# First pass of a decoder trunk on one core: scale's dot product ahead of shift's, weight low parts in two pieces, squares summed by TensorE

## The chip, the cores and the metric

One core of a Trainium2 chip runs the whole program in one launch. The metric is the device time in microseconds (us). Engines are named as the profile names them: PE is TensorE's matmul, PEld its weight load, DVE is VectorE, ACT is ScalarE, POOL is GpSimd, SP is SyncE, which here issues nearly all transfers.

## The reference

Two decoder layers over 256 tokens of width 1024, each a token mixer and a gated ConvFFN. Every sub-layer takes a normed and modulated input `h`, and the change concerns the first of them:

```
mod = silu(c) @ w_ada[i] + b_ada[i]
sh1, sc1, g1, sh2, sc2, g2 = split(mod, 6)
h = rmsnorm(x, norm_mix[i]) * (1.0 + sc1) + sh1
y = dilated_mixture(h, w_in_a, w_out_a, rel_bias)      # starts with h @ w_in_a
```

So before the first projection can start, the kernel needs the root mean square of x, and, for each of eight slices of 128 channels, a shift and a scale, which are dot products of `silu(c)` with 128 columns of `w_ada` each.

## The kernel before

Channels lie on partitions. `x`, `h` and all activations are kept as eight tiles (kt = 0 to 7) of 128 channels by 256 tokens. For accuracy every float32 product of the projections is made as three: operand a is split into a high part (ScalarE's copy into the type fp32r) and a low part (VectorE's subtraction a - high), and `mm3` issues high*high, high*low and low*high into the same accumulator.

The first pass is the projection that makes q, k and v of the first two head pairs. For it, each tile kt brings two transfers, both into the pool `wraw` (four buffers shared by all kinds of weights, so a load waits until the load four places earlier has been used up):

- `ada_chunk(0, kt)` (L130 to L151): 1 MB of `w_ada`, which holds the shift weights of tile kt in its first half and the scale weights in its second (`ADA_ORDER`, L51). Two VectorE dot products (L138), each followed by a small ScalarE activation that makes the column `mod` (shift at L148, scale at L146).
- `split(I["w0"][kt])` (L156 to L170): 0.96 MB of projection weights, 1920 columns. ScalarE copies two halves of 960 columns into `whi` (L165), then VectorE subtracts twice into `wlo` (L169). `wspl` has three buffers of each.

`normed` (L250 to L263) makes h for a tile: VectorE multiplies x by scale and the reciprocal root `rstd` (`xr`, L257), ScalarE adds the shift (`hhi`, L259), VectorE makes `hlo` (L260). TensorE then does for that tile 42 matmuls: 18 of 256 columns for the first head pair (`pqk`, weight columns 0 to 767), 6 of 384 columns for v (columns 768 to 1151, which span both halves), and 18 for the second head pair (columns 1152 to 1919).

Ahead of that stand the squares of x: VectorE squares tiles 0 to 3 (L354), ScalarE tiles 4 to 7 (L357), VectorE adds each four to one by two additions (L360), and `rstd_of` (L183 to L192) sums the two over channels with two matmuls by a matrix of ones (`ms`, L187), then ln and exp on ScalarE (L189, L191). `keep_warm` (L266 to L270) issues matmuls whose result nobody reads.

Each engine runs its own queue strictly in the order in which the program was laid out. A scheduler lays it out from the order of the code and its own estimate of times; `with behind(i)` makes it place what follows after instruction i on its engine. For the tiles from 2 on VectorE's queue is: two dots of tile kt+1, `hlo` of tile kt, both low parts of tile kt+1, `xr` of tile kt+1.

After the pass come the second pair's v (`pv`, weights `in_wv`), the attention of pair 0, and so on.

Of the kernel before, what the change touches and what calls it, by code (L numbers as in the profile page):

```python
# [57 lines left out]
def trunk(ctx: ExitStack, tc: tile.TileContext, I, out):  # L58
# [40 lines left out]
    def col(at):  # L99
        return small[:, at : at + 1]  # L100
# [25 lines left out]

    mod = {}

    def ada_chunk(l, n, dmas=1):
        raw = wraw.tile([P, 2048], F32, tag="raw", name="ada_raw")  # L130
        for i in range(dmas):
            c = slice(2048 * i // dmas, 2048 * (i + 1) // dmas)
            nc.sync.dma_start(raw[:, c], I["w_ada"][l, n][:, c])
        for s in range(2):
            piece, kt = ADA_ORDER[2 * n + s]
            dot = tmp.tile([P, 1], F32, tag="dot", name="dot", bufs=4)
            w = raw[:, D * s : D * s + D]
            nc.vector.tensor_tensor_reduce(  # L138
                w, w, c_bc, op0=ALU.mult, op1=ALU.add, scale=1.0, scalar=0.0, accum_out=dot,
            )  # L140
            m = state.tile([P, 1], F32, tag=f"mod{l}{piece}{kt}", name="mod")
            b = col(C_BADA + 48 * l + 8 * piece + kt)
            if piece in (1, 4):
                g = col((C_NMIX if piece == 1 else C_NFFN) + 8 * l + kt)
                b1 = (16 if piece == 4 else 0) + 8 * l + kt
                last = nc.scalar.activation(m, dot, AF.Identity, scale=g, bias=one_b[:, b1 : b1 + 1])  # L146
            else:
                last = nc.scalar.activation(m, dot, AF.Identity, bias=b)  # L148
            mod[l, piece, kt] = m
        return last  # L150


    last_load, copied, last_lo = [None], [None], [None]

    def split(src, n, dmas=1, after=((), ()), late=(), low=()):
        raw = wraw.tile([P, 2048], F32, tag="raw", name="raw")  # L156
        for i in range(dmas):
            c = slice(n * i // dmas, n * (i + 1) // dmas)
            last_load[0] = nc.sync.dma_start(raw[:, c], src[:, c])
        hi = wspl.tile([P, 2048], F32R, tag="whi", name="whi")  # L160
        lo = wspl.tile([P, 2048], F32R, tag="wlo", name="wlo")
        for i in range(0, n, n // 2):
            c = slice(i, i + n // 2)
            with behind(*after[i > 0]):
                copied[0] = nc.scalar.copy(hi[:, c], raw[:, c])  # L165
        for i in range(0, n, n // 2):
            c = slice(i, i + n // 2)
            with behind(*(late if i else low)):
                last_lo[0] = nc.vector.tensor_tensor(lo[:, c], raw[:, c], hi[:, c].bitcast(F32), op=ALU.subtract)  # L169
        return hi, lo  # L170

    def mm3(ps, a, b, start, stop):

# [76 lines left out]
                st.enter_context(tc.issue_after(i.ins))  # L250
            yield

    def normed(l, sub, r, kt):

        xr = tmp.tile([P, T], F32, tag="xr", name="xr")
        a, sh = mod[l, 3 * sub + 1, kt], mod[l, 3 * sub, kt]
        nc.vector.scalar_tensor_tensor(xr, x[kt], a[:, 0:1], r, op0=ALU.mult, op1=ALU.mult)  # L257
        hi, lo = h_hi[kt][:, :], h_lo[kt][:, :]
        i = nc.scalar.activation(hi, xr, AF.Identity, bias=sh[:, 0:1])  # L259
        j = nc.vector.scalar_tensor_tensor(  # L260
            lo, xr, sh[:, 0:1], hi.bitcast(F32), op0=ALU.add, op1=ALU.subtract
        )
        chain[kt] = chain[7] = i, j  # L263
        return h_hi[kt], h_lo[kt]

# [60 lines left out]
    def parts(w, at, n=P):  # L326
        return w[0][:, at : at + n], w[1][:, at : at + n]
# [27 lines left out]
    with behind(silu):  # L355
        for i in (4, 6):
            last_sq = nc.scalar.activation(sq[:, i : i + 2, :], x_all[:, i : i + 2, :], AF.Square)  # L357
    for n in (0, 4):
        for m in (2, 1):
            last_add = nc.vector.tensor_tensor(sq[:, n : n + m, :], sq[:, n : n + m, :], sq[:, n + m : n + 2 * m, :], op=ALU.add)  # L360
        if n == 0:
            with behind(last_add):
                last_add = scale_terms(0)
    exp_ln_after(last_sq)
    r = rstd_of([sq[:, 0, :], sq[:, 4, :]])

    rows_ps, at = [], 0
    with behind(norm_ops[0]):
        keep_warm(3)
        for i, (g, n) in enumerate(ROWS):  # L370
            c = slice(at, at + n)
            ps = bank("rows", "t")[:16, 0:n]
            rows_ps.append((ps, c))
            mm(ps, tab[:, 16 * g : 16 * g + 16], oh[:33, c], start=True, stop=True)
            at += n
    first = norm_ops[1], last_add
    w0, h = [], []
    for kt in range(KT):
        with behind(*first):
            term = ada_chunk(0, kt, dmas=1 if kt else 2)  # L380
        h.append(normed(0, 0, r, kt))
        if kt:
            w0.append(split(I["w0"][kt], 15 * P))
        else:
            with behind(chain[0][1]):
                w0.append(split(I["w0"][kt], 15 * P, 2, after=((term,), (chain[0][0],))))
# [3 lines left out]
            first = (last_lo[0],)  # L390
        if kt == 1:
            scale_terms(1)
    with tc.issue_after(last_load[0].ins):
        nc.sync.dma_start(x_all, I["xT"])
        nc.sync.dma_start(rows_d, rows)
# [109 lines left out]
    for u in range(NPAIR):  # L505
        with tc.issue_after(last_load[0].ins):
            bias = load_bias(u)
        q = [q_pair[u % 2]]
        k = [[att.tile([P, T + 4], F32R, tag=f"k0{i}", name="k") for i in range(2)]]
        for z in k[0]:  # L510
            nc.gpsimd.memset(z[:, T:].bitcast(F32), 0.0)
        for g in (1, 2):
            q.append(att.tile([P, T], F32, tag=f"q{g}", name="q"))
            k.append(att.tile([P, T], F32, tag=f"k{g}", name="k"))
        v = [att.tile([P, NG * P], F32, tag=f"v{t}", name="v") for t in range(2)]
        if u == 0:
            b0 = [bank("pqk", tg) for tg in "ssspp"]
            pqk = [b[:, T * i : T * i + T] for b in b0[:3] for i in range(2)]
            pv = b0[3:]
            b1 = [bank("pqk", "t") for _ in range(3)]  # L520
            pqk1 = [b[:, T * i : T * i + T] for b in b1 for i in range(2)]
            for kt in range(KT):
                s, e = kt == 0, kt == KT - 1
                for i in range(2 * NG):
                    mm3(pqk[i][:, :T], parts(w0[kt], P * i), h[kt], s and i % 2 == 0, e and i % 2 == 1)
                wv = parts(w0[kt], 6 * P, NG * P)
                for t in range(2):
                    ht = [y[:, P * t : P * t + P] for y in h[kt]]
                    mm3(pv[t][:, : NG * P], ht, wv, s, e)
                for i in range(2 * NG):  # L530
                    mm3(pqk1[i], parts(w0[kt], 9 * P + P * i), h[kt], s and i % 2 == 0, e and i % 2 == 1)
        if u < 2:
            for g in range(NG):
                evacuate(q, k, g, (pqk, pqk1)[u][2 * g], (pqk, pqk1)[u][2 * g + 1])
        else:
            for g in range(NG):
                w = split(I["wqk"][u - 2, g], 2048)
                pqk = bank("pqk", "p")
                pq, pk = pqk[:, :T], pqk[:, T:]
                for kt in range(KT):  # L540
                    s, e = kt == 0, kt == KT - 1
                    mm3(pq[:, :T], parts(w, 2 * P * kt), h[kt], s, False)
                    mm3(pk[:, :T], parts(w, 2 * P * kt + P), h[kt], False, e)
                with behind(evacuate(q, k, g, pq, pk)):
                    next_ada()
        if u > 0:
            pv = [bank("pv", "p") for _ in range(2)]
            for half in range(2):
                with behind(*chain[7]):
                    w = split(I["wv"][u - 1, half], 1536)  # L550
                for k4 in range(4):
                    kt = 4 * half + k4
                    wv = parts(w, 384 * k4, 384)
                    for t in range(2):
                        ht = [y[:, P * t : P * t + P] for y in h[kt]]
                        mm3(pv[t][:, :384], ht, wv, kt == 0, kt == KT - 1)
        for n in range(2):
            by_group(v[n], pv[n], n)
        attend(u, q, k, v, bias)
        if u == 1:  # L560
            for n in range(2):
                next_ada()
# [506 lines left out]
```

## Time and profile before

| | |
|---|---|
| median of three runs | 788.61 us |
| the three runs | 788.61, 790.08, 784.72 us |
| the profiled execution: its time | 784.46 us |
| its span | 782.7 us |
| its mean granted TensorE clock | 0.997 |

| engine | busy us | share of the span |
|---|---|---|
| PEld | 741.9 | 95% |
| DVE | 643.2 | 82% |
| ACT | 480.2 | 61% |
| POOL | 14.4 | 2% |

A share is an average over the whole span; the stage that the change touches lies in its first 60 us and has to be read by itself. In the rows of a timeline the first number is the start, the second the duration, then engine, line, operation, output and input; what stands in brackets is the idle time of the engine before it and what ended it. Vector and scalar instructions overlap a little at their ends, so what one costs its queue is the distance between starts, not the duration.

### The profile page before, as it was taken

The numbers are of one execution on the slowest core, as the hardware profiler recorded it, in microseconds if no ns is written. First come the engines' busy times: TensorE is split into PE (matmuls) and PEld (weight loads), VectorE is DVE, ScalarE is ACT, GpSimd is POOL, SyncE is SP. The second block draws the span as 40 slices with busy tenths as digits, with TensorE's granted clock in tenths as the row PEclk, the third lists the DMA queues.
The fourth block names the chain that finished last, engine by engine and source line by source line (L and its number), as shares of the span: only waits on it lengthen the run. The fifth ranks groups of instructions, "written<-read, shape, count | busy, mean of one in ns | idle before, by whom it ended". The sixth has DMA issues, their size and how long they took to land.

```text
span 782.7 us, 15883 instructions
## 1 busy us (share of the span) xinstructions
PE 769.9 (98%) x6416; PEld 741.9 (95%) x6416; DVE 643.2 (82%) x1160; ACT 480.2 (61%) x936; POOL 14.4 (2%) x40
## 2 busy tenths in 40 slices
PE   8999999999999999999999999999999999999997
PEld 6899999999999999999999999898999999999997
DVE  6998978878779758999998976797568898899762
ACT  5566555545645557867666656664667866667552
POOL 1000000000000010000000100000010000000000
PEclk9999999999999999999999999999999999999999
DMA  9998577585785736777645994966445765556741
GB/s 349 417 325 350 191 287 272 195 323 193 264 299 194 266 103 250 247 268 265 227 144 206 322 341 152 340 241 229 144 144 185 252 211 173 207 182 208 262 158 54
DMA packets 32616, 184.72 MB, mean 236 GB/s; under 512 B 5852, under 2 KB 7388, under 8 KB 16286
## 3 DMA queue, kind: packets, MB, share of 16 engines
q1 hardware_dynamic: 32160, 183.26, 65.4%
q8 instruction: 50, 0.82, 0.4%
q10 hardware_dynamic: 382, 0.45, 0.2%
q14 instruction: 24, 0.20, 0.1%
HBM read 182.59 MB, written 1.10 MB: 235 GB/s over the span
## 4 chain that ended last, share of the span: by engine, by line
PE 74%; DVE 11%; DMA 8%; ACT 4%; issue 2%; ACTq 0%; DVEq 0%
PE pab L176 10%; PE pab L175 10%; PE pab L177 10%; PE pd L177 5%; PE pd L176 5%; PE pd L175 5%; DMA raw<-in_wqk 5%; DVE wlo L169 4%; PE pqk L177 3%; PE pqk L176 3%; PE pqk L175 3%; DMA raw<-in_wv 3%; DVE ada_raw L138 2%; PE py L175 2%; PE py L177 2%
## 5 line engine op out<-in xcount | busy, mean ns | idle before, releaser
L169 DVE TENSOR_TENSOR wlo<-raw,whi 128x1024 fp32r<-128x1024 f32 (+3 forms) x274 | 291.8, 1096 | 52.5 <-ACT whi L165 51.8
L165 ACT CAST whi<-raw 128x1024 fp32r<-128x1024 f32 (+3 forms) x274 | 245.5, 945 | 135.3 <-PE pab L176 40.4
L177 PE MATMUL pab<-hhi,wlo 128*128 128x256 f32 x672 | 184.7, 276 | 0.0
L176 PE MATMUL pab<-hlo,whi 128*128 128x256 f32 x672 | 184.6, 276 | 0.0
L175 PE MATMUL pab<-hhi,whi 128*128 128x256 f32 x672 | 183.2, 277 | 0.0
L176 PEld LDWEIGHTS pab<-hlo,whi 128*128 128x128 f32 x672 | 126.0, 188 | 0.2
L177 PEld LDWEIGHTS pab<-hhi,wlo 128*128 128x128 f32 x672 | 126.1, 188 | 0.0
L175 PEld LDWEIGHTS pab<-hhi,whi 128*128 128x128 f32 x672 | 125.1, 188 | 0.1
L176 PE MATMUL pqk<-hlo,whi 128*128 128x256 f32 x440 | 123.0, 283 | 0.5 <-DVE hlo L260 0.5
L175 PE MATMUL pqk<-hhi,whi 128*128 128x256 f32 x440 | 120.5, 285 | 1.9 <-ACT hhi L259 1.4
L177 PE MATMUL pqk<-hhi,wlo 128*128 128x256 f32 x440 | 122.3, 282 | 0.0
L138 DVE CUSTOM_DVE_ANT_0 ada_raw<-ada_raw,c_bc 128x1024 f32<-128x1024 f32 x96 | 113.4, 1218 | 9.5 <-DMA ada_raw<-in_w_ada 9.5
L177 PE MATMUL pd<-ghi,wlo 128*128 128x256 f32 x352 | 97.1, 276 | 0.0
L176 PE MATMUL pd<-glo,whi 128*128 128x256 f32 x352 | 97.1, 276 | 0.0
L175 PE MATMUL pd<-ghi,whi 128*128 128x256 f32 x352 | 96.8, 276 | 0.0
L175 PEld LDWEIGHTS pqk<-hhi,whi 128*128 128x128 f32 x440 | 81.7, 190 | 3.2 <-ACT hhi L259 1.9
L176 PEld LDWEIGHTS pqk<-hlo,whi 128*128 128x128 f32 x440 | 83.3, 190 | 1.3 <-DVE hlo L260 0.9
L177 PEld LDWEIGHTS pqk<-hhi,wlo 128*128 128x128 f32 x440 | 83.1, 190 | 0.9 <-issue 0.7
L176 PEld LDWEIGHTS pd<-glo,whi 128*128 128x128 f32 x352 | 66.1, 188 | 0.0
L177 PEld LDWEIGHTS pd<-ghi,wlo 128*128 128x128 f32 x352 | 66.1, 188 | 0.0
L175 PEld LDWEIGHTS pd<-ghi,whi 128*128 128x128 f32 x352 | 65.9, 188 | 0.0
L641 ACT ACTIVATE r<-pab,small 128x256 f32<-128x256 f32 x86 | 46.7, 559 | 15.6 <-DVE r L644 15.5
(207 smaller groups left out, 1302.9 us busy)
## 6 DMA issues: line engine op xcount, KB each, us to landing
ada_raw<-in_w_ada SPq DMA_DIRECT2D x47, 1024.0 KB, 6.8
raw<-in_w_up SPq DMA_DIRECT2D x42, 1024.0 KB, 5.0
raw<-in_w_down SPq DMA_DIRECT2D x32, 704.0 KB, 4.8
raw<-in_wqk SPq DMA_DIRECT2D x18, 1024.0 KB, 7.2
raw<-in_wv SPq DMA_DIRECT2D x14, 768.0 KB, 4.5
raw<-in_w SPq DMA_DIRECT2D x7, 960.0 KB, 7.0
raw<-in_w_out_a SPq DMA_DIRECT2D x4, 1024.0 KB, 6.4
raw<-in_w_v_b SPq DMA_DIRECT2D x4, 1024.0 KB, 6.4
```

What stands on the lines that cost most here:

```text
L138: nc.vector.tensor_tensor_reduce(w, w, c_bc, op0=ALU.mult, op1=ALU.add, scale=1.0, scalar=0.0, accum_out=dot,)
L165: copied[0] = nc.scalar.copy(hi[:, c], raw[:, c])
L169: last_lo[0] = nc.vector.tensor_tensor(lo[:, c], raw[:, c], hi[:, c].bitcast(F32), op=ALU.subtract)
L175: mm(ps, a[0], b[0], start=start, stop=False)
L176: mm(ps, a[0], b[1], start=False, stop=False)
L177: return mm(ps, a[1], b[0], start=False, stop=stop)
L641: nc.scalar.activation(r, u[:, :T], AF.Identity, scale=cw[2], bias=col(C_CB + 44 * l + f))
```

## The change

1. `ADA_ORDER` swaps the two halves of each of the first eight chunks: scale's weights come first. So scale's dot product is made before shift's.
2. `ada_chunk` is taken apart into `ada_load` and `ada_dot`; `split` gets a form (`lows=False`) that makes only the high part, and `low_part(w, i)` makes one half of the low part.
3. The loop over tiles is written out in a new order, with the order tied down by `behind`.
4. Squares: VectorE adds only tiles 0 to 3 (two additions fewer); `rstd_of` gets five operands in place of two, so that TensorE adds tiles 4 to 7 itself.
5. `keep_warm(6)` is added after the three matmuls of `rows`.
6. For tile 0 the matmuls of the first head pair are issued as high*high and high*low for all six outputs first, then low*high.

```diff
-ADA_ORDER = [x for kt in range(KT) for x in ((0, kt), (1, kt))]
+ADA_ORDER = [x for kt in range(KT) for x in ((1, kt), (0, kt))]
...
-    for n in (0, 4):
-        for m in (2, 1):
-            last_add = nc.vector.tensor_tensor(sq[:, n : n + m, :], sq[:, n : n + m, :], sq[:, n + m : n + 2 * m, :], op=ALU.add)
-        if n == 0:
-            with behind(last_add):
-                last_add = scale_terms(0)
+    for m in (2, 1):
+        last_add = nc.vector.tensor_tensor(sq[:, 0:m, :], sq[:, 0:m, :], sq[:, m : 2 * m, :], op=ALU.add)
+    with behind(last_add):
+        last_add = scale_terms(0)
...
-    r = rstd_of([sq[:, 0, :], sq[:, 4, :]])
+    r = rstd_of([sq[:, i, :] for i in (0, 4, 5, 6, 7)])
...
+    with behind(last_row):
+        keep_warm(6)
     w0, h = [], []
+    ada = ada_load(0, 0, 2)
+    with behind(norm_ops[1], last_add):
+        dots = [ada_dot(0, 0, s, ada) for s in range(2)]
     for kt in range(KT):
-        with behind(*first):
-            term = ada_chunk(0, kt, dmas=1 if kt else 2)
-        h.append(normed(0, 0, r, kt))
-        if kt:
-            w0.append(split(I["w0"][kt], 15 * P))
...
+        term = dots[1][1]
+        def between(scaled, high):
+            w0.append(split(I["w0"][kt], 15 * P, 1 if kt else 2, after=((term,), (high,)), lows=False))
+            with behind(scaled):
+                return [low_part(w0[-1], 0)]
+        h.append(normed(0, 0, r, kt, (dots[1][0],), between))
+        last = chain[kt][1]
...
+        if kt < KT - 1:
+            ada = ada_load(0, kt + 1)
+            with behind(last):
+                dots = [ada_dot(0, kt + 1, 0, ada)]
+            last = dots[0][0]
+        with behind(last):
+            last = low_part(w0[kt], 1)
...
+        if kt < KT - 1:
+            with behind(last):
+                dots.append(ada_dot(0, kt + 1, 1, ada))
```

In the new `normed`, `between` is called after `xr` and `hhi` have been issued and before `hlo`: `after=((term,), (high,))` puts the first half of the high copy behind shift's small activation (`term`) and the second behind `hhi` (`high`). The program as laid out has, for a tile kt from 2 on:

```
VectorE:  xr(kt), low a(kt), hlo(kt), scale dot(kt+1), low b(kt), shift dot(kt+1)
ScalarE:  scale mod(kt), shift mod(kt), high a(kt), hhi(kt), high b(kt)
```

where the program before has, on ScalarE, shift mod, both copies, scale mod, `hhi` for the later tiles. The planner's queues behind the first pass shift too. On SP, the load of the second half of `in_wv` is issued after the reload of x (`in_xT`, which waits for the last `xr`) and after eight bias loads; before, it was issued ahead of all of them. On VectorE the low parts of that half stand among the evacuations of q and k, not ahead of them.

More of the change, by code (lines that the diff above doesn't have):

```diff
@@ L133, in ada_chunk, with ada_dot, split @@
             nc.sync.dma_start(raw[:, c], I["w_ada"][l, n][:, c])
-        for s in range(2):
[L135 to L150, printed above, removed]
+        return raw
+    def ada_dot(l, n, s, raw):
+        piece, kt = ADA_ORDER[2 * n + s]
+        dot = tmp.tile([P, 1], F32, tag="dot", name="dot", bufs=4)
+        w = raw[:, D * s : D * s + D]
+        i = nc.vector.tensor_tensor_reduce(
+            w, w, c_bc, op0=ALU.mult, op1=ALU.add, scale=1.0, scalar=0.0, accum_out=dot,
+        )
+        m = state.tile([P, 1], F32, tag=f"mod{l}{piece}{kt}", name="mod")
+        b = col(C_BADA + 48 * l + 8 * piece + kt)
+        if piece in (1, 4):
+            g = col((C_NMIX if piece == 1 else C_NFFN) + 8 * l + kt)
+            b1 = (16 if piece == 4 else 0) + 8 * l + kt
+            j = nc.scalar.activation(m, dot, AF.Identity, scale=g, bias=one_b[:, b1 : b1 + 1])
+        else:
+            j = nc.scalar.activation(m, dot, AF.Identity, bias=b)
+        mod[l, piece, kt] = m
+        return i, j
+    def ada_chunk(l, n):
+        raw = ada_load(l, n)
+        for s in range(2):
+            ada_dot(l, n, s, raw)
     last_load, copied, last_lo = [None], [None], [None]
-    def split(src, n, dmas=1, after=((), ()), late=(), low=()):
+    def split(src, n, dmas=1, after=((), ()), late=(), low=(), lows=True):
         raw = wraw.tile([P, 2048], F32, tag="raw", name="raw")
@@ L165, in split @@
                 copied[0] = nc.scalar.copy(hi[:, c], raw[:, c])
+        if not lows:
+            return hi, lo, raw, n // 2
         for i in range(0, n, n // 2):
```

44 lines of the change are left out of this document (29 added, 15 removed).

## The prediction

> **What bounds the kernel.** The page comes first: TensorE is busy nearly throughout.
>
> ```profile
> PE 769.9 (98%) x6416; PEld 741.9 (95%) x6416; DVE 643.2 (82%) x1160; ACT 480.2 (61%) x936; POOL 14.4 (2%) x40
> ```
>
> So the change can win only where TensorE idles or runs slowly, and a delay that it makes in front is hard to win back. Then busy time by stretches, cut at the tiles of the first pass:
>
> ```profile
> 0.00:12.90 12.90, 10.04 (x28) 5.52 (x28) 6.63 (x16) 7.50 (x13) 2.69 (x14) 1.00 0.87 313
> 12.90:17.07 4.17, 4.16 (x20) 4.06 (x21) 4.17 (x6) 1.95 (x5) 0.00 (x0) 0.60 1.00 415
> 20.99:26.20 5.21, 4.72 (x35) 4.52 (x36) 5.21 (x9) 2.87 (x5) 0.00 (x0) 1.00 1.02 421
> 26.20:31.40 5.20, 5.20 (x44) 5.20 (x44) 5.20 (x9) 2.88 (x5) 0.00 (x0) 1.00 1.02 416
> ...
> 775.00:780.00 5.00, 2.42 (x20) 1.95 (x18) 1.99 (x4) 2.26 (x5) 0.00 (x0) 1.00 0.32 122
> 780.00:782.70 2.70, 0.00 (x0) 0.00 (x0) 0.00 (x0) 0.00 (x0) 0.00 (x0) 0.82 0.44 162
> ```
>
> The columns are the stretch, its length, the busy time of PE, PEld, DVE, ACT and POOL, the granted clock, the DMA share and GB/s. Three things are to be seen. In a steady tile (26.20 to 31.40) PE and VectorE are both busy all 5.20 us, with the transfers at a share of 1.02: three resources are full at once, and whatever adds idle time to VectorE becomes the pass's length. The clock was about half from some 13.7 to 17.1 us (0.60 on average in the second row). And of the 12.8 us that PE is idle in all (782.7 - 769.9), 2.9 lie ahead of 12.90 and 5.3 in the last 7.7 us, so that some 4.6 are left in between.
>
> What those are in the first 60 us, the list of waits says:
>
> ```profile
> PE pqk L175 <- ACT hhi L259: 1.4, 2, 0.9
> PE pqk L176 <- DVE hlo L260: 0.5, 1, 0.5
> ```
>
> That 1.9 us is all that better order could return in the waits of the pass itself. The chain of waits agrees: it leaves VectorE at 23.14 and then runs on TensorE alone to the end of the pass.
>
> ```profile
> 23.14 0.39 PE pqk L176
> ...
> 53.60 0.53 PE pqk L175 x4
> ...
> 58.81 0.18 PE pv L175
> ```
>
> The last tile's products begin at 53.60 and the pass ends at 58.81: a tile is 5.21 us of TensorE.
>
> **Part 1: the steady tile.** VectorE's queue for one tile before, by starts:
>
> ```profile
> 35.85 0.48 DVE L257 SCALAR_TENSOR_TENSOR xr<-x_all,mod,rstd 128x256 f32<-128x256 f32 x1
> 36.24 1.22 DVE L138 CUSTOM_DVE_ANT_0 ada_raw<-ada_raw,c_bc 128x1024 f32<-128x1024 f32 x1
> ...
> 37.39 1.22 DVE L138 CUSTOM_DVE_ANT_0 ada_raw<-ada_raw,c_bc 128x1024 f32<-128x1024 f32 x1
> ...
> 38.53 0.48 DVE L260 SCALAR_TENSOR_TENSOR hlo<-xr,mod,hhi 128x256 fp32r<-128x256 f32 x1
> 38.93 2.22 DVE L169 TENSOR_TENSOR wlo<-raw,whi 128x960 fp32r<-128x960 f32 x2
> 41.07 0.47 DVE L257 SCALAR_TENSOR_TENSOR xr<-x_all,mod,rstd 128x256 f32<-128x256 f32 x1
> ```
>
> 0.39 for `xr`, 1.15 and 1.14 for the dots, 0.40 for `hlo`, 2.14 for two low parts: 5.22 with no gap, because between the copies and their use there stands other work. The change keeps all of these and so VectorE's busy time. It changes what precedes what. Now `xr` follows shift's dot, and the first low part follows `xr`; but that low part needs the first half of `whi`, which ScalarE has queued behind shift's small activation, which needs the same shift dot. The waiting instruction holds VectorE's whole queue: `hlo`, the next dots, the second low part; and TensorE waits for them. Its price is from ScalarE's rows:
>
> ```profile
> 26.45 1.00 ACT L165 CAST whi<-raw 128x960 fp32r<-128x960 f32 x1 [0.28 <-DMA raw<-in_w]
> ...
> 37.51 0.30 ACT L148 ACTIVATE mod<-dot,small 128x1 f32<-128x1 f32 x1 [0.63 <-DVE dot L138]
> 37.71 1.87 ACT L165 CAST whi<-raw 128x960 fp32r<-128x960 f32 x2
> ```
>
> The first dot's successor started at 37.39 and the activation at 37.51: 0.12. The copy starts 0.20 later and takes 1.00. With 0.03 for the handover, the low part starts 1.35 after the shift dot; `xr` covers 0.39 of it. The gap is 0.95 us for each tile; a tile lasts 5.22 + 0.95 = 6.17. Bounds: 0.65, if the copy costs only the second half's 0.87 and the activation hides; 1.2 with a little more handover. The nearest rows give 0.95, which I take. TensorE with 5.21 in 6.17 is no longer the bound of the pass.
>
> **Part 2: the front.**
>
> ```profile
> 5.93 2.08 PE L270 MATMUL warm<-ones_d 128*128 128x128 f32 x8
> 7.80 2.33 PE L187 MATMUL ms<-sq,ones_d 128*128 128x256 f32 x4
> 9.92 1.02 PE L270 MATMUL warm<-ones_d 128*128 128x128 f32 x6
> ...
> 10.17 0.47 ACT L189 ACTIVATE ln<-ms,eps 128x256 f32<-128x256 f32 x1 [1.20 <-PE ms L187]
> 10.68 0.42 ACT L191 ACTIVATE rstd<-ln 128x256 f32<-128x256 f32 x1
> ...
> 7.70 1.15 DVE L360 TENSOR_TENSOR sq<-sq 128x512 f32<-128x512 f32 x2 [0.25 <-ACT sq L357]
> 8.77 1.22 DVE L138 CUSTOM_DVE_ANT_0 ada_raw<-ada_raw,c_bc 128x1024 f32<-128x1024 f32 x1
> ...
> 11.60 0.48 DVE L257 SCALAR_TENSOR_TENSOR xr<-x_all,mod,rstd 128x256 f32<-128x256 f32 x1 [0.46 <-ACT mod L146]
> ```
>
> Removed: two VectorE additions, 1.07 us (7.70 to 8.77). But they weren't what the first dot lacks next: its weights. Each of the two loads of the first chunk:
>
> ```profile
> L133 SPq DMA_DIRECT2D ada_raw<-in_w_ada x1: 845/845/845, 2.1 to 2.1; - x1
> ...
> DMA to landing us min/median/max: 7.4/7.4/7.4
> ```
>
> The second half lands at 2.1 + 7.4 = 9.5; the second dot began a dot's 1.14 after the first, at 9.91. At most 0.4 us is won there, and `rstd` comes later anyhow. Added: three `ms` matmuls. Two took 2.33 with a wait of about 0.3 between, a little over 0.84 each as they are issued; three more at that rate are 2.5 us. The warm rows show the clock changing underneath: 8 records in 2.08, then 6 in 1.02, so that it doubled around 10.3. Five from 7.80, three at 0.84 and two at 0.42, and 0.2 of drain, end near 11.4; before, 10.13. With the clock up all the time +0.4, half all the time +2.1; I take +1.2. Scale's activation now precedes shift's and saves 0.18 there, so the first `xr` starts at 11.60 + 1.2 - 0.18 = 12.6.
>
> [...]
>
> From there VectorE: up to the copy's end 1.1 (0.20 and 1.00, less the overlap), low a 1.07, `hlo` 0.40, scale dot 1.15, low b 1.07, shift dot 1.14. Tile 1's shift dot ends at 12.6 + 5.9 = 18.5.
>
> The first `hhi` ends near 14.1 (0.20 + 0.87 + 0.51 after 12.6; 1.87 - 1.00 is what a copy costs the queue). The six `keep_warm` matmuls just ahead of it on TensorE take 2.0 us by the row at 9.92 (two records each) or 3.1 by that at 5.93, so they can hold it up by 3.1 at most. Their cover is the slack of 0.96 us per tile from part 1, which takes that back within four tiles. Without part 1's gap they would cost what they overrun. The order of tile 0's matmuls: nothing, by the same cover.
>
> **Part 3: the tail and the sum.**
>
> ```profile
> 48.98 0.48 DVE L260 SCALAR_TENSOR_TENSOR hlo<-xr,mod,hhi 128x256 fp32r<-128x256 f32 x1
> ...
> 51.52 0.48 DVE L257 SCALAR_TENSOR_TENSOR xr<-x_all,mod,rstd 128x256 f32<-128x256 f32 x1
> ...
> 52.03 0.51 ACT L259 ACTIVATE hhi<-xr,mod 128x256 fp32r<-128x256 f32 x1 [1.72 <-DVE xr L257]
> ```
>
> Before, tile 7's last dot ended at 48.98 and the pass at 58.81, 9.83 later. Now `hhi` comes soon after the dots: 0.12 + 0.20 + 0.87 + 0.51, so TensorE starts tile 7 at 1.7 after the dot. It does three products (0.35) and waits about 0.55 for the second half copy (which ends near 2.6), then goes on: 1.7 + 5.21 + 0.55 = 7.5. The dot itself: 18.5 + 6 x 6.17 + 0.1 (`scale_terms`, moved) = 55.6. The pass ends at 55.6 + 7.5 = 63.1, against 58.81: **+4.3 us**. In short: +0.8 by tile 1's dot, +5.8 in six tiles, -2.3 in the tail.
>
> Behind the pass, SP's queue: the second `in_wv` load now stands behind the reload of x and eight bias loads.
>
> ```profile
> 52.02 0.34 SPq L394 DMA_DIRECT2D x_all<-in_xT  x1
> ...
> raw<-in_wv SPq DMA_DIRECT2D x1, 768.0 KB, 6.0
> ```
>
> The reload waits for the last `xr`, at about 56; with the bias loads the weights are issued near 57.5 and land near 63.5. TensorE needs them after 24 matmuls of the first half at 0.18, near 67: covered by some 1.5 us after copy and subtraction. Should that cover go, the 2 to 3 us come on top. TensorE has almost no idle time later in which to take 4 us back, so I carry them to the end: 784.46 + 4.3 = 788.8 for an execution like the profiled one. That one is 4.15 under the median, whose three runs span 5.4 us; on the median it is 788.61 + 4.3 = **793**.
>
> **Rivals.** *The copy hides and TensorE remains the bound.* If the first half of `whi` were ready when `xr` ends, the tile would stay at 5.21. First `hhi` at 14.1, eight tiles of 5.21 at full clock and some 1.0 of waits end the pass at 56.8: -2.0, **786.6**. It decides at a copy and activation of 0.4 us together; the rows say 1.2. For it speaks that the half-clock stretch (3.4 us, 1.7 of work) may go. [...] Chance 0.15.
>
> *VectorE falls behind for good, slower by over 1%.* Its low parts of tile 7 end at 55.6 + 3.9 = 59.5, 8.0 later than before (51.5, where the last `xr` starts), and 1.8 us of low parts of `in_wv` now stand among the evacuations, ahead of four dots. If attention then starts by VectorE and not by TensorE, all 8.0 are carried, and 1 to 2 for late transfers: +9, **798**. It decides if VectorE's lag of 8.0 stays over TensorE's 4.3 by more than VectorE idles in between. Against it, TensorE has 48 products of `pv` to do first, 48 x 0.18 = 8.6 us. Chance 0.15.
>
> *TensorE's clock falls in the gaps.* One such window of 3.4 us costs up to 1.7 us, several +9: **798** too. Against it, 0.49 us of idle in the row from 20.99 left the clock at 1.00. Chance 0.05.
>
> **The numbers.** My forecast holds 0.65: bounds 0.65 and 1.2 of the gap move the sum by -1.8 and +1.5, `ms` by -0.8 and +0.9; together 791 to 795.5, and the runs' own spread of 2.7 on either side makes 788.5 to 798. Taking in the first rival (786.6, less about one for spread) and the lower half of the others, the range is 785.5 to 799. About 1% (7.9 us) is what a measurement of this kernel can tell from no change. Faster by that is beyond all the idle time at stake: 0.03. Slower by that: the last two rivals and the forecast's upper end, 0.22. Same: 0.75.
>
> **What would show it.** Right: VectorE idle about 0.95 us ahead of each first low part, ended by ScalarE's `whi`; tiles 6.1 to 6.2 us apart; `ln` near 11.4; `pv` starting near 63. Wrong: tiles 5.2 apart, or `pv` before 59. If `pv` starts near 63 and the end is not some 4 us later, the carrying fails, not the pass.

## The result, and the profile after

The changed kernel takes 797.98 us (median of six runs, 797.02 to 799.3). The kernel before takes 787.56 us, the median of its six runs; three of them are those of the table above. The ratio is 1.0133, with a 95% interval of 1.0110 to 1.0156: the change costs 10.4 us. The profiled execution of the changed kernel took 798.04 us with a span of 796.2, against 784.46 and 782.7 before.

The totals of the page mislead: VectorE's busy time is the same to the last digit, and PE's has grown by 9.5 us, though its work has hardly changed.

```profile
PE 779.4 (98%) x6434; PEld 747.9 (94%) x6434; DVE 643.2 (81%) x1158; ACT 481.5 (60%) x936; POOL 14.3 (2%) x40
```

VectorE's timeline of one steady tile of the first pass, in the changed kernel (start, duration, engine, line, operation; in brackets the idle time before it and what ended it):

```profile
25.86 0.48 DVE L273 SCALAR_TENSOR_TENSOR xr<-x_all,mod,rstd 128x256 f32<-128x256 f32 x1
27.18 1.16 DVE L184 TENSOR_TENSOR wlo<-raw,whi 128x960 fp32r<-128x960 f32 x1 [0.85 <-ACT whi L172]
28.26 0.48 DVE L277 SCALAR_TENSOR_TENSOR hlo<-xr,mod,hhi 128x256 fp32r<-128x256 f32 x1
...
32.01 0.48 DVE L273 SCALAR_TENSOR_TENSOR xr<-x_all,mod,rstd 128x256 f32<-128x256 f32 x1
```

and ScalarE's of the next tile:

```profile
32.13 0.30 ACT L150 ACTIVATE mod<-dot,small 128x1 f32<-128x1 f32 x1 [1.82 <-DVE dot L140]
32.33 0.98 ACT L172 CAST whi<-raw 128x960 fp32r<-128x960 f32 x1
33.22 0.51 ACT L275 ACTIVATE hhi<-xr,mod 128x256 fp32r<-128x256 f32 x1
```

The first low part starts 1.32 after `xr`, which takes 0.40 of the queue: VectorE stands idle until the copy is there. Tiles are 6.15 apart (25.86 to 32.01), 5.2 before. Busy time by stretches for the next tile (stretch, length, busy time of PE, PEld, DVE, ACT and POOL, granted clock, DMA share, GB/s):

```profile
32.01:38.17 6.16, 5.73 (x44) 5.32 (x43) 5.31 (x9) 2.86 (x5) 0.00 (x0) 1.00 0.92 340
```

PE is put down as busy for 5.73 of 6.16 us with the same 42 products that took 5.20. A row of 256 columns counts as busy for 0.28 us in the timeline, though the next one starts 0.11 to 0.12 later (53.95 and 54.07, say), so that a part of every pause counts as busy and hides the idle time. `pv` starts at 64.27; before, at 58.65. That is +5.6 us by the end of the pass.

The other half of the loss lies directly behind. SP's issues in the changed kernel:

```profile
49.83 0.42 SPq L429 DMA_DIRECT2D rows_d<-rows  x1
...
55.19 0.52 SPq L362 DMA_DIRECT2D bias<-rows_d  x1
...
59.05 0.54 SPq L428 DMA_DIRECT2D x_all<-in_xT  x1
59.63 1.04 SPq L362 DMA_DIRECT2D bias<-rows_d  x1
60.72 0.60 SPq L363 DMA_DIRECT2D bias<-rows_d  x1
61.41 0.54 SPq L166 DMA_DIRECT2D raw<-in_wv  x1
```

What waits for that last load, by the timelines of ScalarE, VectorE and TensorE in turn:

```profile
67.45 1.56 ACT L172 CAST whi<-raw 128x768 fp32r<-128x768 f32 x2 [2.38 <-DMA raw<-in_wv]
```

```profile
68.31 1.82 DVE L178 TENSOR_TENSOR wlo<-raw,whi 128x768 fp32r<-128x768 f32 x2 [2.66 <-ACT whi L172]
```

```profile
64.27 0.34 PE L190 MATMUL pv<-whi,hhi 128*128 128x384 f32 x1
...
66.18 0.34 PE L192 MATMUL pv<-whi,hlo 128*128 128x384 f32 x1
68.33 0.44 PE L190 MATMUL pv<-whi,hhi 128*128 128x384 f32 x1 [1.81 <-ACT whi L172]
69.33 0.45 PE L191 MATMUL pv<-wlo,hhi 128*128 128x384 f32 x1 [0.55 <-DVE wlo L178]
```

And the stretches around it:

```profile
66.35:69.76 3.41, 1.04 (x4) 0.62 (x4) 1.45 (x2) 2.25 (x5) 0.00 (x0) 1.00 1.00 424
69.76:73.17 3.41, 3.41 (x13) 3.41 (x12) 3.35 (x7) 1.53 (x5) 0.00 (x0) 0.50 1.02 430
```

All three engines stand still for the one transfer, issued at 61.41 and used at 67.45; and for the 3.41 us that follow the granted clock is 0.50 and TensorE's products start 0.32 us apart, not 0.17, which costs another 1.7 (half of 3.41). Only 12 products of `pv` stand ahead of the one that waits (64.27 to 66.18, 0.17 us apart). The first half of the weights feeds 24, so the other 12, which need nothing of the late load, were laid behind the waiting one.

The lag behind the kernel before, measured at the same matmul of each trace, is 5.6 us at the start of `pv`, 10.3 at the first scores (tile `s`), 11.7 at 171 us of the kernel before, and 11.7 still at 734 us. So 10.3 of the 11.7 us are made in two places before 75 us and carried to the end; the prediction had the first place and the carrying. The other 1.4 come by 171 us, and no run locates them. Another 1.8 us that this execution shows in its last 40 us are not in the trace of e_slack, which has much the same losses up to 75 us (see the last section).

### The profile page after: what moved, and what is told of

Read it like the earlier page. It is cut to its first block, busy times and chain, and to the rows that moved or that the text cites. A ratio compares the mean times of both kernels' runs of the same rounds, so it can differ in the third digit from the quotient of the medians.

```text
span 796.2 us, 15933 instructions
## 1 busy us (share of the span) xinstructions
PE 779.4 (98%) x6434; PEld 747.9 (94%) x6434; DVE 643.2 (81%) x1158; ACT 481.5 (60%) x936; POOL 14.3 (2%) x40
## 4 chain that ended last, share of the span: by engine, by line
PE 77%; DVE 10%; DMA 7%; ACT 3%; issue 1%; ACTq 0%; DVEq 0%
PE pab L190 10%; PE pab L192 10%; PE pab L191 10%; PE pd L192 5%; PE pd L190 5%; PE pd L191 5%; DMA raw<-in_wv 3%; DVE wlo L178 3%; PE pqk L190 3%; PE pqk L192 3%; PE pqk L191 3%; DMA raw<-in_wqk 3%; DVE ada_raw L140 3%; PE pv L191 2%; PE pv L190 2%; ACT whi L172 2%
## 5 line engine op out<-in xcount | busy, mean ns | idle before, releaser
L178 DVE TENSOR_TENSOR wlo<-raw,whi 128x1024 fp32r<-128x1024 f32 (+2 forms) x258 | 273.7, 1092 | 54.6 <-ACT whi L172 53.4
L190 PE MATMUL pqk<-hhi,whi 128*128 128x256 f32 x434 | 118.9, 285 | 1.6 <-ACT hhi L275 0.6
L192 PE MATMUL pqk<-hhi,wlo 128*128 128x256 f32 x434 | 118.7, 281 | 0.0
L191 PE MATMUL pqk<-hlo,whi 128*128 128x256 f32 x434 | 118.6, 281 | 0.0
L190 PEld LDWEIGHTS pqk<-hhi,whi 128*128 128x128 f32 x434 | 80.1, 188 | 3.8 <-ACT hhi L275 2.5
L192 PEld LDWEIGHTS pqk<-hhi,wlo 128*128 128x128 f32 x434 | 80.6, 188 | 0.8 <-issue 0.7
L191 PEld LDWEIGHTS pqk<-hlo,whi 128*128 128x128 f32 x434 | 80.7, 188 | 0.3
```

Of the source, the lines that this page charges most:

```text
L190: mm(ps, a[0], b[0], start=start, stop=False)
L191: mm(ps, a[0], b[1], start=False, stop=False)
L192: return mm(ps, a[1], b[0], start=False, stop=stop)
```

## The experiments

Ratios are to the kernel before, run beside each on the same chip. "Lag" is how much later than in the trace of before the same matmul starts.

**e_load: the second `in_wv` load issued early.** Both loads are emitted straight behind the loop, ahead of x's reload and the bias loads.

```diff
...
+    raw_wv = []
+    for half in range(2):
+        raw_wv.append(wraw.tile([P, 2048], F32, tag="raw", name="raw"))
+        with tc.issue_after(last_load[0].ins):
+            last_load[0] = nc.sync.dma_start(raw_wv[half][:, 0:1536], I["wv"][0, half])
+    with tc.issue_after(last_load[0].ins):
+        nc.sync.dma_start(x_all, I["xT"])
...
```

> The changed kernel with one thing undone behind the pass: the load of the second half of in_wv is issued on SP ahead of the reload of x and of the bias loads, as in the kernel before. Theory A (two separate losses: the pass is 5.6 us longer by the gap ahead of each first low part, and the late load costs another 4 to 5 us by a stall of TensorE and the half clock after it): the pass still ends near 64.3 us with tiles 6.16 us apart, the 1.8 us wait of pv for whi goes, no half-clock stretch near 70 us, and the time falls by 4 to 5 us to about 793.5, ratio to the kernel before about 1.007. Theory B (VectorE's lag of 8 us behind the pass is what is carried; the late load is only the place where it shows): the stall moves to a wait for VectorE, and the time stays at 797 to 798, ratio 1.013.

Measured: 792.43 us, ratio 1.0070 (1.0054 to 1.0086). Tiles are still 6.16 apart, the clock never falls between 13 us and the end (its mean is 1.000), and `pv` waits 0.53 us for an evacuation only:

```profile
65.78 0.44 PE L191 MATMUL pv<-whi,hhi 128*128 128x384 f32 x1 [0.53 <-ACT v L541]
```

The late load with what it draws after it is worth 5.0 us (1.0133 to 1.0070 of 787; by the two intervals some 2 us more or less), half of the loss. The planner also laid `pv` otherwise here, with 41 of its 48 products ahead of the first scores; the 5.0 hold that too.

**e_copy: the first half copy no longer behind shift's activation, but behind scale's.**

```diff
-        term = dots[1][1]
+        term = dots[1 if kt == 0 else 0][1]
```

> The changed kernel with the first half of each tile's high copy (from tile 1 on) tied behind scale's small activation in place of shift's, so that ScalarE copies while VectorE still works on the low part and the shift dot. The planner then lays the second in_wv load ahead of the reload of x by itself. Theory A: VectorE's gap ahead of the first low part goes, tiles are 5.2 us apart, the pass ends at 58 to 59 us, no late load, and the time is that of the kernel before within 2 us (786 to 790), ratio 0.998 to 1.003. Theory B: the same for the pass. Theory C (the pass is slow for another reason, such as TensorE waiting for the second half copy, or the order of the low parts): tiles stay above 5.6 us apart and the time above 793.

Measured: 791.99 us, ratio 1.0056 (1.0034 to 1.0078): worse than expected. In this program the planner issues the second `in_wv` load ahead of the bias loads by itself, so that both suspected costs should have been gone. The gap of 0.85 is; but the tiles are 5.3 to 6.4 apart, not 5.2. SP's, ScalarE's and VectorE's timelines of e_copy show what came in its place:

```profile
22.75 0.33 SPq L166 DMA_DIRECT2D raw<-in_w  x1
...
34.16 0.33 SPq L166 DMA_DIRECT2D raw<-in_w  x1
```

```profile
29.10 1.00 ACT L172 CAST whi<-raw 128x960 fp32r<-128x960 f32 x1 [1.40 <-DMA raw<-in_w]
...
35.77 1.00 ACT L172 CAST whi<-raw 128x960 fp32r<-128x960 f32 x1 [2.29 <-DMA raw<-in_w]
```

```profile
31.83 1.23 DVE L140 CUSTOM_DVE_ANT_0 ada_raw<-ada_raw,c_bc 128x1024 f32<-128x1024 f32 x1
...
32.98 1.16 DVE L184 TENSOR_TENSOR wlo<-raw,whi 128x960 fp32r<-128x960 f32 x1
```

The copy now waits for the tile's own weights. A load goes out at 22.75, its data is copied from 29.10 on, and when the second low part has ended the next load goes into the buffer, at 34.16: 11.4 us for a buffer. Two of the four buffers serve these weights, which makes 5.7 us for a tile on average. In that hold stands a dot of 1.15 us between the two low parts, which the change put there.

**e_adj: that dot moved out from between the low parts.** e_copy, and the second low part directly behind `hlo`:

```diff
+        with behind(last):
+            last = low_part(w0[kt], 1)
         if kt < KT - 1:
...
-        with behind(last):
-            last = low_part(w0[kt], 1)
```

> The changed kernel with the first half copy behind scale's activation (as in e_copy), and with the second low part directly behind hlo, ahead of both dots of the next tile, so that the dots are adjacent again. Theory (buffer): in e_copy the tile is 5.5 to 6 us long because a weight buffer is held 1.15 us longer when a dot stands between the two low parts: 6.35 us from issue to landing plus 5.06 from landing to release is 11.4 for two tiles, 5.7 each. With the dots adjacent the hold is some 3.7 to 4, the round trip 10.2, and VectorE's 5.2 bounds again: no copy waits more than 0.3 us for its transfer in the tiles from 2 on, xr 5.2 to 5.35 us apart, pass ends near 60.5, ratio to before 1.001 to 1.003 (only the front's 1.3 to 1.8 us are left). Rival (transfers are simply slower with this order of loads): copies still wait 1 to 2 us for the transfer, ratio 1.0056 as in e_copy.

Measured: 787.97 us, ratio 1.0021 (1.0005 to 1.0038). The waits for the weights are gone but for 0.2 us at one tile, and VectorE's `xr` come in step:

```profile
30.18 0.48 DVE L273 SCALAR_TENSOR_TENSOR xr<-x_all,mod,rstd 128x256 f32<-128x256 f32 x1
35.55 0.48 DVE L273 SCALAR_TENSOR_TENSOR xr<-x_all,mod,rstd 128x256 f32<-128x256 f32 x1
40.92 0.48 DVE L273 SCALAR_TENSOR_TENSOR xr<-x_all,mod,rstd 128x256 f32<-128x256 f32 x1
```

5.37 apart; `pv` starts at 60.2. That is what the theory of the buffer had forecast. The profiled execution is the slowest of the twelve (793.21 us), by losses that lie behind 235 us, so its first 75 us alone are read here.

**e_slack: the same move, but with the gap left in.** The changed kernel with only the diff of e_adj above.

> The changed kernel with the second low part ahead of both dots, as in e_adj, but with the first half copy left behind shift's activation. If the gap by that copy sets the tile, the shorter hold of the weight buffer brings nothing: VectorE idles 0.85 us ahead of each first low part, tiles 6.1 to 6.2 us apart, ratio 1.011 to 1.015 as for the change. If the hold of the buffers had a part in the 6.16, the tiles come to 5.6 to 6.0 and the ratio to 1.008 or less.

Measured: 796.63 us, ratio 1.0136 (1.0105 to 1.0166), 0.85 us idle ahead of each first low part, tiles 6.17 apart. So no cost of the longer hold can be told as long as the gap sets the tile; it is a second bound just below the first.

**e_sq: the squares added by VectorE as before**, with two `ms` matmuls; the rest as changed.

> The changed kernel with the squares added as before: two more additions on VectorE, two ms matmuls in place of five. If the three extra matmuls delay rstd, as the prediction has it, ln starts 1.2 to 2.2 us earlier than 12.47 (c_row's arrival taken off), the first xr too, and as the pass is set by VectorE from there the pass ends that much earlier; the time falls by 1 to 2 us, to about 796.5. If the front is covered by something else (the second half of the first ada load, the copy of whi), the first xr moves by less than 0.5 and the time stays at 798.

Measured: 797.29 us, ratio 1.0128 (1.0079 to 1.0176), four runs from 792.65 to 803.95. The first `xr` starts at 11.41 in place of 13.71, but tile 1's at 18.24 in place of 19.60: VectorE had to wait for tile 1's scale weights.

```profile
14.87 1.22 DVE L140 CUSTOM_DVE_ANT_0 ada_raw<-ada_raw,c_bc 128x1024 f32<-128x1024 f32 x1 [0.83 <-DMA ada_raw<-in_w_ada]
```

A later tile's weights cost it 0.68 more, and `pv` started at 63.7, only 0.6 sooner. In the profiled execution it then waited longer for the late load (3.3 us), and a half-clock stretch of 6.83 us followed. No gain can be told.

**e_warm: without the six `keep_warm` matmuls.**

```diff
-    with behind(last_row):
-        keep_warm(6)
```

> The changed kernel without the six added keep_warm matmuls. If VectorE sets the pass, nothing changes in the time (798, within 1 us) even if the granted clock falls to half for one 3.4 us window near the start of the pass. If TensorE's clock matters in the pass, the pass ends up to 1.7 us later and the time is 799 to 800.

Measured: 797.09 us, ratio 1.0128 (1.0114 to 1.0142): nothing that can be told. `pv` starts at 63.6, 0.7 us sooner, which is by how much the input `c_row` came sooner in this execution (2.29 in place of 2.98).

**e_adj_sq: e_adj with the squares as before.**

> e_adj with the squares added by VectorE as before (two ms matmuls in place of five). If the front's delay of the first hhi (1.3 to 1.8 us) is what e_adj has left over the kernel before, it goes: first xr near 11.4, pass ends 58.5 to 59.3, ratio 0.999 to 1.001. Rival: tile 1's scale weights land no sooner, as in e_sq, and the front's gain is lost again: ratio as in e_adj, 1.001 to 1.003.

Measured: 784.38 us, ratio 0.9979 (0.9966 to 0.9992): faster than both kernels, by 1.7 us than the one before. `pv` starts at 58.3. Where the gap bound the pass (e_sq) no worth of the squares could be told; here they come to 3.3 us (1.0021 to 0.9979, each ratio known to some 1 us), of which the two profiles show 1.9 at the end of the pass. What keeps the tile at 5.37 and not VectorE's 5.22 is seen on VectorE and ScalarE of e_adj_sq:

```profile
35.70 0.48 DVE L277 SCALAR_TENSOR_TENSOR hlo<-xr,mod,hhi 128x256 fp32r<-128x256 f32 x1
36.24 1.16 DVE L184 TENSOR_TENSOR wlo<-raw,whi 128x960 fp32r<-128x960 f32 x1
```

```profile
35.22 0.99 ACT L172 CAST whi<-raw 128x960 fp32r<-128x960 f32 x1
```

The second copy ends at 36.21, and the second low part starts 0.54 after `hlo` where 0.40 would do.

**e_nowarm: e_adj_sq without `keep_warm(6)`.**

> e_adj_sq without the six keep_warm matmuls. In e_adj_sq the first product starts at 15.0, straight behind the last of them, though its hhi is there from about 13.1: with the slack of 0.96 us per tile gone, they should now cost what they overrun, as far as VectorE does not bound the pass. Theory A (VectorE with 5.37 us per tile bounds, TensorE catches up by 0.16 per tile and half of it is hidden): first product near 13.5, pass end 0 to 0.7 earlier, ratio 0.997 to 0.998. Theory B (TensorE carries all of it): ratio 0.996. Theory C (without them the clock falls to half while TensorE waits for hhi and the first tile is slower): ratio 0.999 to 1.002.

Measured: 786.25 us, ratio 0.9987 (0.9969 to 1.0005). The first product starts 1.4 us sooner, at 13.59; the lag against e_adj_sq is -0.4 by 29 us and -0.1 at `pv`. The difference between the two kernels, 0.0008, is inside both intervals: neither a price nor a use of these matmuls can be told.

**b_tsq: one part of the change alone on the kernel before**, four of the squares added by TensorE, without two of VectorE's additions.

```diff
...
-    r = rstd_of([sq[:, 0, :], sq[:, 4, :]])
+    r = rstd_of([sq[:, i, :] for i in (0, 4, 5, 6, 7)])
```

> The kernel before with one part of the change alone: TensorE adds four of the squares (five ms matmuls, two VectorE additions fewer). Theory: ms at half clock end 1.3 to 2 us later, the first hhi and the whole pass with them; ratio 1.0015 to 1.0025, pass end +1.2 to +1.8. Rival: tile 1 waits for its transfers anyway, so that the delay is taken up there: ratio 1.000, pass end within 0.4 of before's 58.7.

Measured: 795.12 us, ratio 1.0112 (1.0099 to 1.0125), far above both theories. The edit isn't alone: in the kernel before VectorE's order in the pass is left to the planner, and with it the queue changed. VectorE's timeline of b_tsq:

```profile
18.28 1.22 DVE L138 CUSTOM_DVE_ANT_0 ada_raw<-ada_raw,c_bc 128x1024 f32<-128x1024 f32 x1
...
19.42 2.22 DVE L169 TENSOR_TENSOR wlo<-raw,whi 128x960 fp32r<-128x960 f32 x2
21.56 1.22 DVE L138 CUSTOM_DVE_ANT_0 ada_raw<-ada_raw,c_bc 128x1024 f32<-128x1024 f32 x1
...
23.85 0.48 DVE L257 SCALAR_TENSOR_TENSOR xr<-x_all,mod,rstd 128x256 f32<-128x256 f32 x1
```

Tile 1's `xr` stands behind both dots of tile 2, so that TensorE had no tile 1 until after 24 us (its clock fell to half at 24.84), and the second `in_wv` load went out at 56.07, behind the bias loads. The run says nothing about the price of the five `ms` matmuls.

**e_late: e_adj_sq with the second `in_wv` load put back behind x's reload and all bias loads.**

> e_adj_sq with one thing put back as the change has it: the second in_wv load stands on SP behind the reload of x and all bias loads. The late load by itself, on a pass that is as fast as before's. In the changed kernel that load was issued 4.8 us after the last xr and the pass ended 7.6 us after it; here the last xr is again some 7.6 us ahead of the pass's end, so the weights land as late against it as there. Theory (late load costs a wait and then a slow stretch of the clock): TensorE waits 1.5 to 3 us for whi in the first pv, a half-clock stretch of about 3.4 us follows, and the kernel is 4 to 5 us slower than e_adj_sq: ratio to before 1.003 to 1.0045. Rival 1 (only the wait counts): 2 us, ratio 1.0005. Rival 2 (the load was covered, and the changed kernel's loss behind the pass came from its VectorE being late): nothing, ratio 0.998 as e_adj_sq.

Measured: 785.24 us, ratio 0.9974 (0.9955 to 0.9992), as fast as e_adj_sq. The load was issued 4.7 us after the last `xr`, as in the changed kernel, and VectorE and ScalarE did wait for it:

```profile
61.47 0.84 ACT L175 CAST whi<-raw 128x768 fp32r<-128x768 f32 x1 [1.82 <-DMA raw<-in_wv]
```

```profile
62.34 0.96 DVE L181 TENSOR_TENSOR wlo<-raw,whi 128x768 fp32r<-128x768 f32 x1 [2.11 <-ACT whi L175]
```

But TensorE did not: here the planner, which knew of the late load, had laid pair 0's 33 score matmuls (61.67 to 64.37) between the halves of `pv`, and the evacuations that those need ahead of the copies. This run does not price the late load by itself, then; it shows that it can be free.

**e_order: the changed kernel with just that order.** SP's queue is unchanged; the scores of pair 0, with the evacuations that they need, stand ahead of the second half of `pv`, and with that all 24 products of the first half stand ahead too, where the changed kernel has 12.

```diff
+                    i, j = keys[0]
+                    w = split(I["wv"][u - 1, half], 1536, **(dict(after=((i,), (i,)), low=(j,), late=(j,)) if u == 1 and half else {}))
...
+                        with behind(*(scored[:1] if u == 1 and kt == 4 else ())):
+                            mm3(pv[t][:, :384], ht, wv, kt == 0, kt == KT - 1)
```

> The changed kernel with its late second in_wv load left where it is (SP's queue is the same), but with TensorE's order behind it changed: the 33 score matmuls of pair 0 (some 2.6 us) stand ahead of the second half of pv, and the evacuations that they need stand ahead of that half's copies and low parts. Theory (the late load costs only because the products that need it stand next in TensorE's queue): the wait of 1.8 + 0.55 us is covered but for 0 to 0.6, no half-clock stretch at 69 to 73, and the lag behind the pass stays at the pass's own 5 to 6 us: ratio 1.006 to 1.008, as e_load's 1.007. Rival 1 (the half-clock stretch comes for another reason than the wait): it is there again, ratio 1.009 to 1.011. Rival 2 (the load costs by itself, wherever its products stand): ratio 1.012 to 1.013.

Measured: 796.65 us, ratio 1.0143 (1.0122 to 1.0165). In its profile the theory's steps are all there: TensorE waits for nothing at 66 to 73 us, the clock stays at 1.00, the lag at 171 us is 5.9. But 2.4 us were lost near 268, at the last pair's `in_wv`, and the median is no better than the change's. So it was run and profiled again:

> e_order a second time, for a second profiled execution and a second median. Its first profile had no wait and no half-clock stretch at 66 to 73 us and a lag behind the kernel before of 5.8 us at 171 us (the change: 11.7), but then lost 2.4 us near 268, where the last pair's pv waited 1.5 + 0.5 us for its own late in_wv load and a half-clock stretch of 3.41 us followed; and its median was no better than the change's. If that second wait is the rule, it is there again and the ratio is 1.010 to 1.0145. If it was a mishap of one run, the end lags by 6 to 8 us and the ratio is 1.007 to 1.010. Either way the lag at 171 us is 5 to 6.5.

Measured: 796.18 us, ratio 1.0122 (1.0094 to 1.0149). The second profile had no loss near 268. It has one at 77 us. VectorE and then TensorE, in e_order_again:

```profile
70.11 1.83 DVE L178 TENSOR_TENSOR wlo<-raw,whi 128x768 fp32r<-128x768 f32 x2 [3.29 <-ACT whi L172]
...
78.42 0.55 DVE L470 CUSTOM_DVE_ANT_0 prob<-s,bias 128x386 f32<-128x386 f32 x1
...
78.90 0.16 DVE L476 TENSOR_SCALAR m<-m 128x2 f32<-128x2 f32 x1
```

```profile
79.13 0.60 PE L451 MATMUL s<-k,q 128*128 128x258 f32 x3 [1.73 <-DVE m L476]
```

```profile
76.38:79.79 3.41, 1.68 (x22) 1.28 (x20) 3.41 (x8) 3.00 (x6) 0.00 (x0) 1.00 1.03 418
79.79:83.21 3.42, 3.42 (x22) 3.30 (x21) 3.34 (x7) 2.25 (x9) 0.00 (x0) 0.50 0.84 307
```

TensorE no longer waits for the weights, but VectorE still does: its low parts of the late load held its whole queue for 3.29 us. The row maxima of the scores (L470) came that much later, TensorE waited 1.73 us for them, and the half-clock stretch came as well. The lag at 171 us is 9.5, not the expected 5 to 6.5. The medians stand nearest to rival 2 of this experiment: the load costs about as much wherever TensorE's products for it stand. This profile shows one way in which it can, by another engine's queue that it blocks. In e_late VectorE waited 2.11 us, and no wait of TensorE came of it.

The first execution of e_order got through at 77 us with a wait of 0.29. The load had gone out sooner there, as SP's rows of e_order and e_order_again show, in this order:

```profile
59.61 0.54 SPq L166 DMA_DIRECT2D raw<-in_wv  x1
```

```profile
62.05 0.54 SPq L166 DMA_DIRECT2D raw<-in_wv  x1
```

and VectorE in e_order waited half as long:

```profile
67.86 1.83 DVE L178 TENSOR_TENSOR wlo<-raw,whi 128x768 fp32r<-128x768 f32 x2 [1.68 <-ACT whi L172]
```

`rows_d` was sent at 49.20 and at 49.38, but the bias loads, which wait for it, began at 53.98 and at 55.78. Why it landed so much later isn't known, and one profile of each is all there is.

## Why the prediction came out as it did

**The gap: right, to a hundredth or two.** 6.17 us per tile were forecast, 6.15 to 6.17 came, with VectorE's idle time ended by `whi` as the text had said (0.85 us in the rows, 0.92 by the distances between starts; 0.95 was forecast). e_copy and e_adj show that the copy's place is the cause.

**The tail: right.** 7.5 us from the last shift dot to the end of the pass; 56.65 to 64.27 is 7.6.

**The front: late by 1.1 us, most of it by something else than `ms`.** The ten rows of the five `ms` matmuls:

```profile
8.53 3.91 PE L202 MATMUL ms<-sq,ones_d 128*128 128x256 f32 x10
```

They took 3.91 us against the 2.33 of the two before: +1.6, where the prediction took +1.2 and bounded it by +0.4 and +2.1. They also began 0.7 us later than before, at 8.53 and not 7.80, because `c_row` had landed 0.7 us later (2.98 and 2.25); e_warm, where it came at 2.29, has its first `xr` at 13.00. So `ln` started at 12.47 (forecast 11.4) and the first `xr` at 13.71 (12.6). These 1.1 us are most of the difference between the +4.3 forecast for the pass and the +5.6 measured; 0.16 is the other mark for its end (58.81 and 58.65 before), and 0.1 the tail. The term differs between executions: the ten rows took 4.41 us in e_load, where `ln` started at 13.03 and `c_row` had landed at 3.0 as here. In the changed kernel the clock went up under them, at 11.74: they start 0.43 us apart up to 11.51, and 0.22 apart from 11.84 on.

**What failed is a cover in part 3:** "the weights are issued near 57.5 and land near 63.5 [...] covered by some 1.5 us". They were issued at 61.41 and were there at 67.45. The last `xr` came near the forecast, at 56.65; but the eight bias loads, at some 0.6 us of SP each, had only begun at 55.19 (they read `rows_d`, which was sent at 49.83). With x's reload they kept SP busy until 61.3, and six of them stood ahead of the reload. The other half of the same step failed too: TensorE needed the load not after 24 products of `pv`, but after 12. Behind 24 of them it would have come to the late weights at 64.27 + 24 x 0.174 = 68.4 (an estimate from these rows), when the first copy of them had just ended, and the wait of 1.81 would have been all but covered. With its cover gone, the load cost the "2 to 3 us" named there (1.81 + 0.55) and, not foreseen for this place, a half-clock stretch of 1.7. e_load measures the whole at 5.0 us.

**The range held the time partly by luck.** The forecast was 793 us. The bounds of its terms end at 795.5 (added straight they are 790.4 and 795.4, not 791 and 795.5); the runs' spread and half of the last two rivals carried the range on to 799. The measured 798.0 lies beyond what the terms could give, because the late load stood among them at nothing. By the prediction's own line of 1% between same and slower the change is slower by 1.3%, an outcome to which it gave 0.22, against 0.75 for same.

**The rivals.** *The copy hides* fell in every tile. *VectorE falls behind for good* gave the right time (798) by luck: its mechanism, VectorE's lag carried as a whole, did not run, since in e_load, with that lag kept, 5.0 us went with the late load. But e_order_again shows VectorE's queue, held by that load, to be close behind TensorE's. *The clock falls in the gaps* named the right price per stretch and the wrong place: with 0.85 us of VectorE's idle time in each tile the clock stayed at 1.00 from 11.74 to 69.76; the one fall, to 0.50 until 73.17, came behind the wait for the late load. `keep_warm`'s cover held (e_warm). That they would cost what they overrun once the gap is gone is not shown: e_nowarm's first product came 1.4 us sooner, and by the end of the pass 0.1 was left.

**The sum, from the runs:** the late load 5.0 us (e_load), the gap and the hold of the buffers 3.9 (e_load to e_adj, 1.0070 to 1.0021; the planner put the load early in e_adj by itself), the squares 3.3 (e_adj to e_adj_sq): about 12 us from 1.0133 to 0.9979. Each of the three is a difference of two ratios and known to about 2 us. What is left of the change in e_adj_sq is worth about 1.7 us: the swap of scale and shift with both copies and low parts where they don't wait, the `keep_warm` matmuls and tile 0's order. Which of them earns it isn't shown. In its profile the pass ends 0.4 us sooner than before (58.26 and 58.65), and the half-clock stretch that the kernel before has from 13.72 to 17.14 is not there.

## What to carry to other kernels

When a dependency is put nearer, work out where the copy that feeds it stands in its own engine's queue, and how long each step's buffer is then held: two bounds within half a microsecond of each other stood behind one another here, and removing the first alone showed little of what the two were worth (1.0070 to 1.0056, then 1.0021). When a load moves in the issue queue, count each small transfer ahead of it (0.6 us apiece here) and what the first of them waits for; a load that landed late was paid here by the queue that reached it with no other work laid ahead (TensorE 1.81 and 0.55 us in the changed kernel, VectorE 3.29 in e_order_again). Issuing it sooner brought 5 us here (e_load), while moving its readers brought nothing that the medians show (e_order). Count, too, how many products the planner really laid ahead of the first reader: 12 here, where the code's order has 24. And in a program laid out by a planner, an edit "alone" may move more than itself (b_tsq, e_late, e_load): compare the queues before reading the time.

## What the runs showed of the hardware

The half-clock stretches in these traces (granted clock 0.50) lasted 3.41 us (13.72 to 17.14 before, 69.76 to 73.17 in the changed kernel) or twice that (6.83, in e_sq), but for the one in which each program ends. The full-clock stretches behind a rise were whole multiples of 3.413 us in both kernels: 58.03 us from the first rise to the fall in the changed kernel (17 times), 764.59 us from 17.14 to the fall at the end in the kernel before (224 times). The first rise lay at 10.31 us before and at 11.74 in the changed kernel. TensorE was not equally busy in the 3.41 us ahead of a fall: not at all in b_tsq (0.00 us from 21.43 to 24.84), hardly in e_sq (one wait of 3.3 us), but 1.04 us in the changed kernel (66.35 to 69.76) and 1.68 in e_order_again, by the rows above, and 2.31 in e_adj:

```profile
263.73:267.14 3.41, 2.31 (x22) 1.63 (x20) 2.66 (x4) 3.09 (x7) 0.00 (x0) 1.00 0.82 327
```

Its waits in those 3.41 us came to 1.19 us (e_adj), 1.73 (e_order_again) and 2.4 in all (the changed kernel). PE's busy time alone doesn't tell what follows: in e_nowarm 3.41 us with 2.71 busy (9.74 to 13.16) were followed by a clock of 1.00, in the kernel before 3.41 us with 2.84 (10.31 to 13.72) by 0.50. What makes the clock fall is not shown by these runs.

The same matmuls also run at two paces at the same granted clock of 1.00. Of the last projection's rows 257 fell into 30 us in the changed kernel's profile, and 268 into 30 us of the same work before:

```profile
757.00:787.00 30.00, 30.00 (x257) 30.00 (x256) 15.72 (x24) 12.65 (x22) 0.00 (x0) 1.00 0.34 118
```

```profile
744.00:774.00 30.00, 30.00 (x268) 30.00 (x266) 15.73 (x24) 12.78 (x22) 0.00 (x0) 1.00 0.30 100
```

That is 0.117 us for one against 0.112. It costs 1.8 us in the last 40 us of that execution, and comes and goes: from 745 to 790 us the trace of e_warm has 397 rows in 44.81 us of busy PE, that of the changed kernel 380. No cause for it was found.
